# A second product in two nested levels of seven-for-eight block products, its weight operands streamed from DRAM

## Chip, cores, metric

One core of a Trainium2 chip runs the whole kernel. The metric is device time in microseconds (us). "Before" is the kernel before the change, "after" the changed kernel.

## The reference

```python
batch, m, k, h, n = 16, 512, 768, 3072, 768          # 8192 rows of x
y = np.matmul(x, w1) + b1
y = 0.5 * y * (1.0 + erf(y / np.sqrt(2.0)))          # GELU
return np.matmul(y, w2).astype(np.float32)
```

Two dense products with a GELU between them. Operands are float16 on the chip, sums float32.

## The kernel before

The rows are worked on in eight blocks of 1024. In each block the first product gives G = gelu(x w1 + b1), and the second gives G w2. Each product is cut into 2 x 2 quarters and made with seven quarter products instead of eight (the scheme of Strassen and Winograd). VectorE makes the sums and differences of operands that the seven products need, and VectorE and ScalarE combine the seven results as they leave PSUM. A "unit" is one set of seven products that share the PSUM banks bX, bY, bZ and bW.

The first product has 12 units a block, each of 7 x 3 matmuls of 512 columns. The second has 4 units, each of 7 x 12 matmuls of 384 columns:

```python
class Unit2:                                # second product, 128 + 128 rows a unit
    F = N2                                  # 384 columns
    C = NH                                  # 12 chunks of the contraction
    def mm(self, p, dst, first, c0, c1):
        ...
        for c in range(c0, c1):
            a = {1: G1[:, c, 0, r], 2: G2[:, c, 0, r], 4: G2[:, c, 1, r],
                 3: GS[3][:, c, :], 5: GS[0][:, c, :], 6: GS[1][:, c, :],
                 7: GS[2][:, c, :]}[p]
            nc.tensor.matmul(out=dst[:, 0:N2], lhsT=a, rhs=w2o[:, slot, c, :], ...)
```

All of w2 and its sums (`w2o`) stays in SBUF. The pieces of w1 are loaded again in every block with a cast on the way, by DMAs that POOL issues, and their sums are made again by VectorE. x is loaded by POOL and turned by DMA transposes that SP issues. These run during the second product of the block before:

```python
# in the second product, unit k, between products ("slots")
if k == 0 and slot == 4:  # load x tiles 0-3 of the next block
if k == 1 and slot == 1:  # DMA-transpose them
if k == 1 and slot == 4:  # load tiles 4-7, and four pieces of w1 (POOL)
if k == 2 and slot == 1:  # transpose tiles 4-7
```

Of the kernel before, what the change touches and what calls it, by code (L numbers as in the profile page):

```python
# [14 lines left out]
PSUM = bass.MemoryType.PSUM  # L15

# [14 lines left out]
def kernel(  # L31
# [25 lines left out]

    wp = ctx.enter_context(tc.tile_pool(name="wp", bufs=1))
    wtp = ctx.enter_context(tc.tile_pool(name="wtp", bufs=4))
    xhp = ctx.enter_context(tc.tile_pool(name="xhp", bufs=4))  # L60
    pwp = ctx.enter_context(tc.tile_pool(name="pwp", bufs=2))
    tmpp = ctx.enter_context(tc.tile_pool(name="tmpp", bufs=2))
    outp = ctx.enter_context(tc.tile_pool(name="outp", bufs=2))
    pp = ctx.enter_context(tc.tile_pool(name="pp", bufs=1, space=PSUM))

    w2o = wp.tile([P, 7, NH, N2], F16, name="w2o")
    G1 = wp.tile([P, NH, 2, RH], F16, name="G1")
    G2 = wp.tile([P, NH, 2, RH], F16, name="G2")
    GS = [wp.tile([P, NH, P], F16, name=f"GS{k}") for k in range(4)]
    XT = wp.tile([P, 2, 2 * KQ, RH], F16, name="XT")  # L70
    XS = [wp.tile([P, KQ, RH], F16, name=f"XS{k}") for k in range(4)]
# [9 lines left out]
    with tc.manual_schedule():  # L81

        soon, queue, late = [], [], []
# [20 lines left out]

        def load_wt(n):
            hi = n % NH
            wt = wtp.tile([P, 7, KQ, P], F16, name="wt")
            wts[n] = wt
            for half in range(2):
                c0 = (half * NH + hi) * P  # L110
                nc.gpsimd.dma_start(  # L111
                    out=wt[:, 2 * half:2 * half + 2, :, :].rearrange("p a k c -> p (a k) c"),
                    in_=w1r[:, :, c0:c0 + P])
# [7 lines left out]

        def prep_wt(n):
            wt = wts[n]
            t_ops(lambda s: wt[:, s, :, :], KQ * P, soon)

        W2C = 3

        def load_w2(q, c):
            slot, r0, n0 = ((B11, 0, 0), (B21, NH, 0), (T1, 0, N2), (B22, NH, N2))[q]
            nc.gpsimd.dma_start(out=w2o[:, slot, c:c + W2C, :],  # L130
                                in_=w2r[:, r0 + c:r0 + c + W2C, n0:n0 + N2])

        def prep_w2(c):
            t_ops(lambda s: w2o[:, s, c:c + W2C, :], W2C * N2, queue, late)
# [3 lines left out]
        def load_x(sb, t):  # L138
            xh = xhp.tile([P, K], F16, name="xh")
            nc.gpsimd.dma_start(out=xh[:], in_=xr[:, sb * 8 + t, :])  # L140
            xhs[t] = xh
# [4 lines left out]
        def transpose_dma(t):  # L146
            nc.sync.dma_start_transpose(out=xT_of(t), in_=xhs[t][:])
# [15 lines left out]
        def x_sums():  # L163
            n = KQ * RH
            later(n, lambda: tt(XS[0][:], A21, A22, ADD))
            later(n, lambda: tt(XS[1][:], XS[0][:], A11, SUB))
            later(n, lambda: tt(XS[2][:], A11, A21, SUB))
            later(n, lambda: tt(XS[3][:], A12, XS[1][:], SUB))

        def g_sum(k, u, c0=0, c1=NH):  # L170
# [5 lines left out]
            later((c1 - c0) * P, lambda: tt(s[k], a, b, op))  # L176


        class Unit1:
# [4 lines left out]
            def __init__(self, g, sb, hi):  # L184
                self.g, self.sb, self.hi = g, sb, hi
                self.wt = wts[sb * NH + hi]
# [9 lines left out]
            def alloc(self):  # L196
                self.tmp = tmpp.tile([P, 2, RH], FP32, name="tmp")
# [7 lines left out]
            def right_done(self):  # L205
                hi = self.hi
                nc.scalar.activation(out=G2[:, hi, :, :], in_=self.tmp[:], func=GELU,  # L207
                                     bias=b1t[:, NH + hi:NH + hi + 1])
# [6 lines left out]
        class Unit2:  # L215
# [7 lines left out]
            def mm(self, p, dst, first, c0, c1):  # L223
                r = slice(self.u * P, (self.u + 1) * P)
                slot = {1: B11, 2: B21, 3: B22, 4: T4, 5: T1, 6: T2, 7: T3}[p]
                for c in range(c0, c1):
# [3 lines left out]
                    nc.tensor.matmul(out=dst[:, 0:N2], lhsT=a, rhs=w2o[:, slot, c, :],  # L230
# [3 lines left out]
            def alloc(self):  # L234
                self.o = outp.tile([P, 2, N], FP32, name="osb")
# [15 lines left out]

        def p1(u, c0, c1):
            u.mm(1, bX[u.g % 2], True, c0, c1)
# [3 lines left out]

        def p7(u):
            u.mm(7, bY[u.g % 2], False, 0, u.C)

        def add_c22(u):
            nc.vector.tensor_tensor(out=u.c22(), in0=bY[u.g % 2][:, 0:u.F],  # L262
                                    in1=u.pw[:, 0:u.F], op=ADD)
# [3 lines left out]

        def copy_w(u):
            u.pw = pwp.tile([P, 512], FP32, name="pw")
            nc.scalar.copy(out=u.pw[:, 0:u.F], in_=bW[:, 0:u.F])  # L270
# [3 lines left out]

        def add_c12(u):
            nc.vector.tensor_tensor(out=u.c12(), in0=bZ[:, 0:u.F], in1=u.pw[:, 0:u.F], op=ADD)  # L276
            u.right_done()
# [7 lines left out]

        def copy_yz(u):
            nc.vector.tensor_copy(out=bZ[:, 0:u.F], in_=bY[u.g % 2][:, 0:u.F])  # L287
# [6 lines left out]
        def period(i, j, fill):  # L294

            turn = isinstance(i, Unit2) and isinstance(j, Unit1)
            if turn:
                p7(j)
                add_c22(j)
                p1(i, 0, 5)  # L300
                p3(j)
                add_c12(j)
# [4 lines left out]
            else:  # L307
# [3 lines left out]
                if j:  # L311
                    p7(j)
                    add_c22(j)
            fill(1)
            if i:
                p5(i)
                copy_w(i)
            fill(2)
            if j and not turn:
                p3(j)  # L320
                add_c12(j)
            fill(3)
            if i:
                p6(i)
                copy_yz(i)
# [32 lines left out]
        x_sums()  # L358
# [4 lines left out]

        units = []
        for sb in range(nsb):
            units += [(1, sb, hi) for hi in range(NH)] + [(2, sb, u) for u in range(NU)]
        w2_loads = [(q, c) for c in range(0, NH, W2C) for q in range(4)]
        prev = None
        for g, (kind, sb, k) in enumerate(units):
            last_sb = sb + 1 == nsb  # L370

            def fill(slot, kind=kind, sb=sb, k=k, last_sb=last_sb):
                if kind == 1:
                    n = sb * NH + k
                    if slot == 1:
                        if k in (5, 9):
                            for s in range(4):
                                g_sum(s, 0, k - 5, k - 1)
                        if k == NH - 1:
                            for s in range(4):  # L380
                                g_sum(s, 0, 8, 10)
                        if k + 1 < NH:
                            prep_wt(n + 1)
                        if sb == 0 and k >= 3 and k % 2 == 1 and (k - 3) // 2 * W2C < NH:
                            prep_w2((k - 3) // 2 * W2C)
                        sums(900)
                    if slot == 4:
                        sums(1500)
                    if slot == 5 and k >= 1 and k + 3 < NH:
                        load_wt(n + 3)  # L390
                    if slot == 5 and sb == 0:
                        for q, c in w2_loads[:2]:
                            load_w2(q, c)
                        del w2_loads[:2]
                    if slot == 6:
                        flush(soon)
                        if k == NH - 1:
                            flush(queue)
                else:
                    if slot == 1:  # L400
                        if k == 0:
                            for s in range(4):
                                g_sum(s, 0, 10, NH)
                        else:
                            g_sum(2, k)
                        flush(queue)
                    if slot == 2 and k + 1 < NU:
                        queue.extend(late)
                        late.clear()
                        g_sum(0, k + 1)  # L410
                    if slot == 3 and k > 0:
                        g_sum(3, k)
                    if slot == 4 and k + 1 < NU:
                        g_sum(1, k + 1)
                    if slot > 1:
                        sums(1200)
                    if not last_sb:
                        if k == 0 and slot == 4:
                            for t in range(4):
                                load_x(sb + 1, t)  # L420
                        if k == 1 and slot == 1:
                            for t in range(4):
                                transpose_dma(t)
                        if k == 1 and slot == 4:
                            for t in range(4, 8):
                                load_x(sb + 1, t)
                            for n in range(4):
                                load_wt((sb + 1) * NH + n)
                        if k == 2 and slot == 1:
                            for t in range(4, 8):  # L430
                                transpose_dma(t)
                        if k == 3 and slot == 2:
                            prep_wt((sb + 1) * NH)
                            x_sums()
                    if slot == 6 and k == NU - 1:
                        flush(queue)
                        flush(soon)

# [34 lines left out]
```

## Time and profile before

| | before |
|---|---|
| median of 3 runs | 905.48 us (905.38 to 906.16) |
| TensorE matmul (PE) busy | 98% of a span of 904.5 us |
| VectorE (DVE), ScalarE (ACT) busy | 58%, 43% |
| mean granted TensorE clock | 0.992 |

Two stretches of the trace, one first product and one second product in the middle of the run. Columns: the stretch, then busy time of each engine with its number of instructions, the granted clock as a share of full speed, the mean busy share of the 16 DMA engines, and GB/s. The DMA share adds up the packets' times, which can overlap, so it can pass 1.

```profile
core 0: us, PE busy (x) PEld busy (x) DVE busy (x) ACT busy (x) POOL busy (x), PEclk, DMA share, GB/s
245.00:299.00 54.00, 54.00 (x255) 24.79 (x254) 39.45 (x89) 37.58 (x57) 15.29 (x20) 1.00 0.75 88
299.00:354.00 55.00, 55.00 (x336) 32.68 (x334) 24.83 (x41) 10.12 (x20) 8.71 (x12) 1.00 0.72 115
```

PE is busy all the time in both. In the second product VectorE is idle for more than half of it, and the DMA engines for about a quarter.

The timeline of PE at the end of the last block shows how far apart the matmuls start: 12 of 384 columns start every 1.95 us.

```profile
888.41 2.11 PE L230 MATMUL bY_93<-w2o,GS_80 128*128 128x384 f16 x12
890.36 2.11 PE L230 MATMUL bY_92<-w2o,G_78 128*128 128x384 f16 x12
```

From such starts, 162.5 ns for 384 columns and 215.9 ns for 512, I take 2.5 ns + 0.417 ns a column. For each pair of neighbouring matmuls, the distance of their starts less this figure is "excess". For the kernel before, the figures add up to 877.9 us and the excess to 21.0 us, 20.5 of it in the start-up and the first block. From the second block on almost nothing is lost: TensorE alone sets the time.

### The profile page before, as it was taken

How to read it: one execution, taken by the hardware profiler on the slowest of the kernel's cores; microseconds unless marked ns; L12 is line 12 of the kernel's file. 1: busy time of each engine (PE TensorE's matmuls, PEld its weight loads, DVE VectorE, ACT ScalarE, POOL GpSimd, SP SyncE). 2: the span in 40 equal slices, each digit the busy share in tenths (PEclk: the TensorE clock that was granted, in tenths of full speed). 3: DMA queues.
4: the chain of work that ended last, by engine and by line, in shares of the span. 5: the costliest groups of instructions: out<-in, count | busy, mean ns of one | idle time of the engine just before them, and what ended most of it. 6: DMA issues, size and time to landing. Idle time of an engine off the chain costs nothing.

```text
span 904.5 us, 12591 instructions
## 1 busy us (share of the span) xinstructions
PE 886.6 (98%) x4764; PEld 465.6 (51%) x4764; DVE 529.0 (58%) x1045; ACT 386.2 (43%) x614; POOL 204.9 (23%) x278
## 2 busy tenths in 40 slices
PE   5999999999999999999999999999999999999998
PEld 2444654456544565445654466544654456544564
DVE  3788446854578436774267734676346764468532
ACT  2665116741177312772137721476115751167411
POOL 5561202321033300333003230132302412022000
PEclk7999999999999999999999999999999999999999
DMA  9997916969179881979439692497915979168011
GB/s 156 119 194 118 160 59 88 98 105 164 56 86 105 102 143 71 88 88 145 100 86 89 89 169 76 79 92 99 169 71 78 87 107 166 54 90 85 1 70 70
DMA packets 223308, 92.06 MB, mean 102 GB/s; under 512 B 200720, under 2 KB 215056, under 8 KB 223248
## 3 DMA queue, kind: packets, MB, share of 16 engines
q0 software_dynamic: 166144, 55.07, 56.1%
q1 hardware_dynamic: 57104, 36.20, 14.9%
q8 instruction: 37, 0.61, 0.3%
q14 instruction: 23, 0.19, 0.1%
HBM read 110.11 MB, written 25.17 MB: 150 GB/s over the span
## 4 chain that ended last, share of the span: by engine, by line
PE 92%; DMA 5%; DVE 1%; POOL 1%; issue 1%; ACT 0%; DVEq 0%; POOLq 0%
PE bY_93 L230 10%; PE bY_92 L230 10%; PE bY_93 L192 9%; PE bY_92 L192 9%; PE bX_90 L230 7%; PE bZ L230 7%; PE bX_91 L230 7%; PE bW L230 7%; PE bW L192 6%; PE bZ L192 6%; PE bX_91 L192 6%; PE bX_90 L192 6%; DMA wt<-in_w_dram 3%; DMA xh<-in_x_dram 1%; DVE wt L86 1%
## 5 line engine op out<-in xcount | busy, mean ns | idle before, releaser
L192 PEld LDWEIGHTS <-wt 128*128 128x128 f16 x2016 | 197.6, 98 | 245.2 <-issue 11.2
L111 POOL DMA_DIRECT2D wt<-in_w_dram x192 | 158.0, 837 | 489.3 <-PE bY_92 L192 344.4
L207 ACT ACTIVATE G_78<-tmp,b1t 128x1024 f16<-128x1024 f32 x96 | 110.2, 1148 | 123.8 <-DVE tmp L276 123.8
L86 DVE TENSOR_TENSOR wt<-wt 128x384 f16<-128x384 f16 x384 | 135.6, 353 | 10.2 <-DMA wt<-in_w_dram 3.3
L270 ACT COPY pw<-bW 128x512 f32<-128x512 f32 (+1 forms) x128 | 71.8, 561 | 112.2 <-PE bW L230 88.4
L230 PEld LDWEIGHTS <-G_78 128*128 128x128 f16 x768 | 75.2, 98 | 50.4
L192 PE MATMUL bW<-XS_84,wt 128*128 128x512 f16 x288 | 78.5, 382 | 4.0 <-DVE wt L86 4.0
L192 PE MATMUL bX_90<-XT,wt 128*128 128x512 f16 x288 | 78.9, 383 | 0.0
L192 PE MATMUL bX_91<-XT,wt 128*128 128x512 f16 x288 | 77.8, 379 | 0.0
L192 PE MATMUL bZ<-XS_87,wt 128*128 128x512 f16 x288 | 77.8, 379 | 0.0
L276 DVE TENSOR_TENSOR tmp<-bZ,pw 128x512 f32<-128x512 f32 x96 | 65.7, 684 | 5.6 <-PE bZ L192 5.6
L262 DVE TENSOR_TENSOR tmp<-bY_92,pw 128x512 f32<-128x512 f32 x48 | 33.2, 691 | 59.4 <-PE bY_92 L192 38.7
L230 PE MATMUL bW<-w2o,GS_79 128*128 128x384 f16 x384 | 67.6, 326 | 0.0
L230 PE MATMUL bZ<-w2o,GS_82 128*128 128x384 f16 x384 | 67.6, 326 | 0.0
L140 POOL DMA_DIRECT2D xh<-in_x_dram x64 | 34.6, 551 | 136.8 <-DMA XT<-xh 116.4
L262 DVE TENSOR_TENSOR osb<-bY_92,pw 128x384 f32<-128x384 f32 x16 | 8.9, 558 | 85.9 <-issue 82.8
L287 DVE COPY bZ<-bY_92 128x512 f32<-128x512 f32 (+1 forms) x64 | 42.6, 666 | 17.3 <-PE bY_92 L230 11.2
L230 PEld LDWEIGHTS <-G_77 128*128 128x128 f16 x384 | 37.6, 98 | 27.4
L262 DVE TENSOR_TENSOR tmp<-bY_93,pw 128x512 f32<-128x512 f32 x48 | 33.0, 688 | 31.4 <-PE bY_93 L192 23.5
L230 PEld LDWEIGHTS <-GS_81 128*128 128x128 f16 x384 | 37.6, 98 | 25.6
L230 PEld LDWEIGHTS <-GS_82 128*128 128x128 f16 x384 | 37.6, 98 | 25.6
L230 PEld LDWEIGHTS <-GS_80 128*128 128x128 f16 x384 | 37.6, 98 | 24.8
(58 smaller groups left out, 1128.5 us busy)
## 6 DMA issues: line engine op xcount, KB each, us to landing
wt<-in_w_dram POOLq DMA_DIRECT2D x192, 192.0 KB, 4.6
out_dram<-osb SPq DMA_DIRECT2D x64, 384.0 KB, 2.3
xh<-in_x_dram POOLq DMA_DIRECT2D x64, 192.0 KB, 5.4
w2o<-in_w_dram POOLq DMA_DIRECT2D x16, 288.0 KB, 8.7
XT<-xh SPq DMA_TRANSPOSE x56, 3.8
b1t<-in_b_dram SPq DMA_DIRECT2D x1, 12.0 KB, 5.3
```

The costliest lines, as they stand in the source:

```text
L86: nc.vector.tensor_tensor(out=o, in0=a, in1=b, op=op)
L111: nc.gpsimd.dma_start(out=wt[:, 2 * half:2 * half + 2, :, :].rearrange("p a k c -> p (a k) c"), in_=w1r[:, :, c0:c0 + P])
L140: nc.gpsimd.dma_start(out=xh[:], in_=xr[:, sb * 8 + t, :])
L192: nc.tensor.matmul(out=dst[:, 0:RH], lhsT=self.wt[:, slot, c, :], rhs=a[:, c, :], start=first and c == 0, stop=c == self.C - 1, skip_group ...
L207: nc.scalar.activation(out=G2[:, hi, :, :], in_=self.tmp[:], func=GELU, bias=b1t[:, NH + hi:NH + hi + 1])
L230: nc.tensor.matmul(out=dst[:, 0:N2], lhsT=a, rhs=w2o[:, slot, c, :], start=first and c == 0, stop=c == self.C - 1, skip_group_check=True)
L262: nc.vector.tensor_tensor(out=u.c22(), in0=bY[u.g % 2][:, 0:u.F], in1=u.pw[:, 0:u.F], op=ADD)
L270: nc.scalar.copy(out=u.pw[:, 0:u.F], in_=bW[:, 0:u.F])
L276: nc.vector.tensor_tensor(out=u.c12(), in0=bZ[:, 0:u.F], in1=u.pw[:, 0:u.F], op=ADD)
L287: nc.vector.tensor_copy(out=bZ[:, 0:u.F], in_=bY[u.g % 2][:, 0:u.F])
```

## The change

The intent is to save matmul time in the second product. From block 3 on, each of its seven quarter products is again cut in four and made with seven products: 49 products of 12 matmuls of 192 columns, 588 x 192 columns where there were 336 x 384. Blocks 1 and 2 keep the old form. During them the 49 operands of w2 are stored in DRAM: VectorE makes 28 of them, and 21 are pieces of operands that were there already. From block 3 on they are streamed through a ring of 15 buffers, 15 loaded during the first product and 34 while the second runs. The pieces of w1 with their sums are kept in DRAM too, and loaded ready-made by SP. To make room, most SBUF buffers are now laid over each other in one `arena`.

The core of the diff (cuts marked):

```diff
+    w1s = [dp.tile([P, 7, KQ, P], F16, name=f"w1s{n}") for n in range(NH)]        # DRAM
+    w2s = {(p, q): dp.tile([P, NQ, N4], F16, name=f"w2s{p}{q}") ...}              # DRAM, 49
+    RING = 15
...
+            if hi in kept:                                   # load_wt, from block 3 on
+                nc.sync.dma_start(out=wt[:], in_=w1s[hi][:])
+                return
...
+        def load_ring(sb, n):
+            if n < 49 and sb < nsb:
+                nc.sync.dma_start(out=ring_of(sb, n), in_=w2s[w2_order[n]][:])
...
+        class Unit3:                                         # 7 of these a block
+            def mm(self, q, dst, first, c0, c1):
+                for c in range(NQ):
+                    for t in range(2):
+                        nc.tensor.matmul(out=dst[:, t * N4:(t + 1) * N4], lhsT=a,
+                                         rhs=w[:, c, :], ...)  # 192 columns
+                load_ring(self.sb, n + RING)
...
+                if self.p == 5:                              # fourth unit
+                    for r in range(2):
+                        tt(par[1][:, r], par[1][:, r], self.dst[:, r], ADD)
+                    for r in range(2):
+                        nc.gpsimd.tensor_tensor(out=self.dst[:, r], in0=par[2][:, r],
+                                                in1=self.dst[:, r], op=ADD)
+                        self.store(r)
...
+            if sb + 1 < nsb:                                 # second product, unit k
+                if k == 0 and slot == 1: load_next_x(sb + 1, range(3))
+                if k == 1 and slot == 4: # DMA-transpose tiles 0-2, load 3-5
+                if k == 3 and slot == 1: # DMA-transpose tiles 3-5, load 6-7
+                if k in (4, 5, 6) and slot == 6:
+                    load_wt((sb + 1) * NH + k - 4)           # first weights of the next block
+                if k == 4 and slot == 4: # DMA-transpose tiles 6-7
```

## The prediction

> **What bounds the kernel now.** TensorE. The page shows PE busy 98% of 904.5 us and granted clock 0.992; the chain that ended last is 92% PE. The timeline of PE shows matmuls packed without gaps: 12 of 384 columns start every 1.95 us (162.5 ns each), 3 of 512 columns every 0.648 us (215.9 ns each). That fits 2.5 ns + 0.417 ns a column. A 1024-row block is 252 matmuls of 512 columns (54.4 us) and 336 of 384 (54.6 us), 109.0 us together, which is also the distance from block to block in the timeline. VectorE 58%, ScalarE 43%, DMA are hidden.
>
> **What the change does.** In blocks 3 to 8 (six of eight) the second product takes 49 products of 12 matmuls of 192 columns: 588 per block instead of 336. My estimate from the fit is 82.5 ns each, 48.5 us a block, so 6.1 us saved per block and 36.5 us in all. This needs each weight load to hide behind only 82.5 ns of streaming. The trace's warm transposes (128 columns, one load each) start about 55 ns apart, but only six in a row. The Trainium skill, "TensorE: Matmul & The Clock Gate", section "Back-to-back issue gap", gives about 81 ns sustained for load and matmul pairs at 128 columns; no run here shows that yet. If true it is just not binding at 192.
>
> **Added costs.**
> - VectorE. The 48 weight sums a block (0.353 us) vanish from block 3 on, and the old activation sums (about 16 us). New, at 0.95 us per 1536 elements: 28 level sums (27 us), half sums and S4 (about 14 us), and five of seven units with six 384-wide evictions of 0.56 us (about 19 us with the rest). About 50 us of that must run inside the 48.5 us second product, about 84 us a block. So VectorE becomes nearly as full as TensorE there; I expect 0 to 3 us of stalls a block, chiefly where the second product begins and ends.
> - DMA. A ring load is 128 x 2304 B. Stores of 3072 B packets took 125 ns (packet times in the trace), so about 95 ns by proportion, 0.76 us per load on 16 engines, against 0.99 us per product. With x loads, transposes and first weights the second product asks for slightly more than the engines' whole time (share about 1.1), but 15 products of prefetch are made in the first product, which absorb a backlog of some 8. First-product weights become large plain loads instead of casting ones (837 ns of POOL each now); that relieves the DMA.
> - Blocks 1 and 2: 28 more splits of about 0.75 us and 49 stores fit VectorE's idle half. The first block's first product already has DMA share 1.18 and loses 2.7 us (stretch view); narrower w2 pieces add about 2 us. Earlier x loads give back about 1 us.
>
> **Sum.** 905.5 - 36.5 + about 6 (VectorE, turns) + about 2 (blocks 1 and 2) = 877 us, 80% between 867 and 891. Faster by over 2% (below 887.4): 0.78; within 2%: 0.18; slower: 0.04.
>
> **What would show it.** 192-column matmuls start 82 to 84 ns apart in the PE timeline; block distance 103 to 105 us from block 3 on; VectorE over 85% busy in those second products, PE waits there naming VectorE lines, few naming the ring's DMA; POOL busy falls by over half.
>
> **What would make it wrong.** Pair pitch above 90 ns (weight load or issue bound): 588 x 7.5 ns x 6 = 26 us lost, gain gone. Ring loads late because stores or transposes sit in front of them in SP's in-order queue (a transpose holds SP about 1.3 us). VectorE's order delaying evictions that free PSUM banks, in every period rather than at the turns.

## The result

The changed kernel takes 932.19 us (median of 4 runs, 928.63 to 933.76) against 905.50: ratio 1.0288, 95% interval 1.0257 to 1.0318. A ratio here is the mean time of one kernel's fast runs over that of the other's of the same rounds, so it is not quite the ratio of the medians. The prediction was 877 us with 867 to 891: wrong, and in the wrong direction.

| | before | after |
|---|---|---|
| span of the profiled run | 904.5 us | 929.7 us |
| sum of matmul figures (2.5 ns + 0.417 ns a column) | 877.9 us | 841.3 us |
| excess | 21.0 us | 82.7 us |
| mean granted clock | 0.992 | 0.977 |

The saving of 36.6 us is there, exactly as estimated. It is overrun by 61.7 us of excess: blocks 4 to 8 begin 111 to 114 us after the block before, where 103 to 105 were predicted. The PE timeline of block 3 shows both (start, us, engine, line, operation, tiles, shapes, count, and in brackets the idle time before it and what ended it):

```profile
350.57 1.15 PE L422 MATMUL bY_144<-arena,G_134 128*128 128x192 f16 x12
351.56 1.15 PE L422 MATMUL bX_143<-arena,G_134 128*128 128x192 f16 x12
352.55 1.15 PE L422 MATMUL bX_142<-arena 128*128 128x192 f16 x12
355.04 1.15 PE L422 MATMUL bY_145<-arena 128*128 128x192 f16 x12 [1.33 <-DVE bZ L515]
...
366.40 1.46 PE L333 MATMUL bX_143<-XT,wt 128*128 128x512 f16 x3 [5.27 <-DMA wt<-w1s_72]
367.66 2.13 PE L422 MATMUL bY_144<-arena 128*128 128x192 f16 x12
369.58 1.49 PE L333 MATMUL bW<-XS_136,wt 128*128 128x512 f16 x3
```

Twelve matmuls start in 0.99 us, 82.5 ns each, with a weight load for every one. Then there is a gap in which PE waits for VectorE's sum into bank bZ, and at the turn into block 4 one of over 5 us in which it waits for the first weights of that block. After it the same twelve matmuls take 1.92 us between starts: TensorE runs at half clock.

PE's waits, longest sums first (us in total, times, longest):

```profile
PE bX_143 L333 <- DMA wt<-w1s_72: 12.9, 3, 5.3
PE bX_142 L333 <- DMA wt<-w1s_72: 8.8, 2, 5.9
PE bY_145 L422 <- DVE bZ L515: 5.4, 6, 1.3
PE bY_144 L422 <- DVE bZ L515: 5.4, 6, 1.3
PE bY_144 L371 <- ACT bY_144 L475: 5.1, 1, 5.1
```

From the starts of the matmuls the 61.7 us of added excess come to:

| where | added us | how counted |
|---|---|---|
| gaps at the turns into blocks 4 to 8 | 22.6 | 5.43 + 3.07 + 5.16 + 6.10 + 2.79 |
| half clock right behind those gaps | 9.4 | 2.40 + 1.30 + 1.46 + 2.71 + 1.56 |
| waits for VectorE in the second and sixth unit, six blocks | 12.8 | 6 x 0.63 and 6 x 1.5 |
| blocks 1 and 2, gaps and half clock | 13.3 | block 3 begins at 252.6 us against 239.3; 5.3 of it one gap in block 2's second product |
| rest of blocks 3 to 8 | 3.6 | remainder |

(The expectations below call the unit of the second wait the fifth. Counted from one, as the second unit is, it is the sixth.)

Why are the weights late? SP's timeline of the later part of block 3's second product (start, us for the issue, what):

```profile
335.20 7.53 SPq L255 DMA_TRANSPOSE XT<-xh  x3
...
350.23 3.33 SPq L255 DMA_TRANSPOSE XT<-xh  x2
353.65 0.55 SPq L239 DMA_DIRECT2D arena<-w2s_99  x1
354.29 1.41 SPq L446 DMA_DIRECT2D out_dram<-arena  x2
355.80 0.49 SPq L239 DMA_DIRECT2D arena<-w2s_104  x1
356.34 0.47 SPq L157 DMA_DIRECT2D wt<-w1s_72  x1
```

In the program the request for the first weights stands right behind the fifth unit's last product, and TensorE was through with that at 345.6 us. SP comes to it 10.7 us later: five transposes held it for 7.53 and 3.33 us, and between them it waited 1.8 us for an x tile. The chain that ended last then has this load as one link of ten microseconds (start, us, link):

```profile
356.34 10.02 DMA wt<-w1s_72
```

Two things are wrong at once. The load is issued only at 356.3 us, when PE needs it at about 361. And it takes 10 us instead of the 4 us that such loads take in the middle of the first product. The stretches of the same block, cut as for the kernel before, show the reason for the latter:

```profile
260.00:311.00 51.00, 51.00 (x239) 23.20 (x238) 31.90 (x54) 38.71 (x61) 0.00 (x0) 1.00 0.60 207
311.00:360.00 49.00, 47.07 (x551) 45.41 (x550) 46.57 (x80) 12.94 (x25) 9.09 (x10) 1.00 0.99 257
...
365.00:371.00 6.00, 4.60 (x19) 2.84 (x20) 0.56 (x1) 0.57 (x1) 0.00 (x0) 0.50 1.04 399
```

In the second product VectorE went from 24.8 us busy to 46.6 of 49, and the DMA engines from a share of 0.72 to 0.99. In slices of 6 us the share is 0.38 at first, and 1.03 to 1.17 from 323 us on. In the first product it is 0.60.

The last line, six microseconds right behind the gap, shows the granted clock at 0.50. The Trainium skill, "TensorE: Matmul & The Clock Gate", section "What's actually happening", says that the clock falls to half after an idle window of about 3.4 us. The traces here agree on the 3.4 us, but show that less idle time is enough. In all sixteen traces the stretches of half clock that do not run into the end of the kernel last 3.41 us or a whole multiple of it (6.83, 13.65), and those at the five turns of this kernel begin 112.64 us apart (364.53, 477.17 and so on), which is 33 slots of 3.413 us. With all traces cut into such slots, and the first 25 us left out, full clock was lost after each of the 44 slots in which PE was idle for 1.98 us or more, and after none of the 4026 with 1.97 us or less (idle by the modelled ends of matmuls). So what a gap costs depends on where it falls: one that left PE idle for 2.04 us in e14_pet_late was followed by half clock, one of 3.5 us in e13_notr_late, cut in two by the edge of a slot, was not.

### The profile page after: what moved, and what is told of

It is laid out like the page before. It is cut to its first block, busy times and chain, and to the rows that moved or that the text cites. A ratio compares the mean times of both kernels' runs of the same rounds, so it can differ in the third digit from the quotient of the medians.

```text
span 929.7 us, 16276 instructions
## 1 busy us (share of the span) xinstructions
PE 869.7 (94%) x6276; PEld 565.6 (61%) x6276; DVE 665.6 (72%) x1151; ACT 417.1 (45%) x680; POOL 116.4 (13%) x146
## 4 chain that ended last, share of the span: by engine, by line
PE 66%; DMA 15%; DVE 12%; ACT 2%; issue 2%; POOL 1%; SPq 1%; DVEq 0%; ACTq 0%; POOLq 0%
PE bY_144 L333 9%; PE bY_145 L333 8%; PE bX_143 L333 6%; DVE arena L127 6%; PE bW L333 5%; PE bX_142 L333 5%; PE bZ L333 5%; DMA wt<-in_w_dram 4%; DMA wt<-w1s_72 4%; PE bY_145 L422 4%; PE bY_144 L422 4%; PE bW L422 3%; PE bZ L422 3%; PE bX_142 L422 2%; PE bX_143 L422 2%
## 5 line engine op out<-in xcount | busy, mean ns | idle before, releaser
L422 PEld LDWEIGHTS <-arena 128*128 128x128 f16 x2664 | 226.0, 99 | 21.1 <-issue 16.6
L348 ACT ACTIVATE G_134<-arena,b1t 128x1024 f16<-128x1024 f32 x96 | 110.3, 1149 | 63.8 <-DVE arena L505 63.8
L127 DVE TENSOR_TENSOR arena<-arena 128x1536 f16<-128x1536 f16 (+5 forms) x176 | 127.7, 746 | 0.9
L482 DVE TENSOR_TENSOR arena<-bY_145,pw 128x512 f32<-128x512 f32 (+1 forms) x52 | 35.4, 681 | 94.9 <-PE bY_145 L333 69.0
L333 PE MATMUL bX_143<-XT,wt 128*128 128x512 f16 x288 | 80.1, 388 | 13.1 <-DMA wt<-w1s_72 12.9
L333 PE MATMUL bX_142<-XT,wt 128*128 128x512 f16 x288 | 80.5, 389 | 8.8 <-DMA wt<-w1s_72 8.8
L505 DVE TENSOR_TENSOR arena<-bZ,pw 128x512 f32<-128x512 f32 (+1 forms) x104 | 70.5, 678 | 19.6 <-PE bZ L333 13.8
L333 PE MATMUL bY_144<-XT,wt 128*128 128x512 f16 x288 | 78.0, 379 | 3.5 <-DVE bZ L520 3.4
L482 DVE TENSOR_TENSOR arena<-bY_144,pw 128x512 f32<-128x512 f32 (+1 forms) x52 | 35.4, 681 | 63.1 <-PE bY_144 L333 35.8
L333 PE MATMUL bY_145<-XT,wt 128*128 128x512 f16 x288 | 77.8, 379 | 2.1 <-DVE bZ L520 1.2
L475 ACT COPY bY_145<-bX_143 128x512 f32<-128x512 f32 (+1 forms) x73 | 39.9, 547 | 83.3 <-DVE arena L454 39.5
L475 ACT COPY bY_144<-bX_142 128x512 f32<-128x512 f32 (+1 forms) x73 | 40.4, 554 | 69.8 <-DVE arena L454 39.6
L422 PE MATMUL bY_144<-arena 128*128 128x192 f16 x612 | 61.7, 253 | 5.4 <-DVE bZ L515 5.4
L422 PE MATMUL bY_145<-arena 128*128 128x192 f16 x612 | 60.5, 250 | 5.4 <-DVE bZ L515 5.4
L371 PEld LDWEIGHTS <-arena 128*128 128x128 f16 x384 | 38.0, 99 | 32.3 <-issue 7.0
L127 DVE TENSOR_TENSOR arena<-arena,G_133 128x1024 f16<-128x1024 f16 (+4 forms) x86 | 48.5, 564 | 1.8
L161 POOL DMA_DIRECT2D wt<-in_w_dram x48 | 39.5, 831 | 79.8 <-DVE wt L127 35.3
```

The lines of the kernel that those rows point to most:

```text
L127: nc.vector.tensor_tensor(out=o, in0=a, in1=b, op=op)
L161: nc.gpsimd.dma_start(out=wt[:, 2 * half:2 * half + 2, :, :].rearrange("p a k c -> p (a k) c"), in_=w1r[:, :, c0:c0 + P])
L333: nc.tensor.matmul(out=dst[:, 0:RH], lhsT=self.wt[:, slot, c, :], rhs=a[:, c, :], start=first and c == 0, stop=c == self.C - 1, skip_group ...
L348: nc.scalar.activation(out=G2[:, hi, :, :], in_=self.tmp, func=GELU, bias=b1t[:, NH + hi:NH + hi + 1])
L422: nc.tensor.matmul(out=dst[:, t * N4:(t + 1) * N4], lhsT=a, rhs=w[:, c, :], start=first and c == 0 and t == 0, stop=c == NQ - 1, skip_grou ...
L475: nc.scalar.copy(out=bY[u.g % 2][:, 0:u.F], in_=bX[u.g % 2][:, 0:u.F])
```

## The experiments

The theories. BANDWIDTH: the DMA engines have too little time in the second product, and whatever is moved, something waits. ORDER: the first weights are late because they stand last in SP's queue. VECTORE FULL: VectorE is the limit there. PORT: POOL's additions slow VectorE.

| run | edit | result | us | ratio to before | 95% |
|---|---|---|---|---|---|
| e1_early | first weights early | correct | 916.5 | 1.0121 | 1.0096 to 1.0147 |
| e2_act | first weights by ScalarE's queue | correct | 964.6 | 1.0638 | 1.062 to 1.0656 |
| e3_noadd | no additions on POOL | wrong | 928.5 | 1.0245 | 1.0222 to 1.0268 |
| e4_actstore | stores of blocks 1, 2 by ScalarE's queue | correct | 933.1 | 1.0312 | 1.0264 to 1.0359 |
| e6_halfring | e1, half of each streamed operand | wrong | 897.4 | 0.9893 | 0.9871 to 0.9915 |
| e7_notr | e1, no DMA transposes | wrong | 897.5 | 0.9896 | 0.9879 to 0.9914 |
| e5_pet | e1, transposes on TensorE | correct | 902.0 | 0.9946 | 0.9928 to 0.9964 |
| e8_dve | e1, VectorE work moved | correct | 916.3 | 1.0105 | 1.0086 to 1.0124 |
| e13_notr_late | no DMA transposes, weights late | wrong | 923.7 | 1.018 | 1.0154 to 1.0206 |
| e10_mix | e1, 5 of 8 transposes on TensorE, block 2 relieved | correct | 926.4 | 1.0205 | 1.0168 to 1.0242 |
| e11_mix_dve | e10 and e8 | correct | 923.5 | 1.0177 | 1.015 to 1.0205 |
| e12_petblock2 | e5, block 2 relieved | correct | 898.5 | 0.9901 | 0.9881 to 0.9922 |
| e14_pet_late | transposes on TensorE, weights late | correct | 910.7 | 1.004 | 1.0022 to 1.0057 |
| e15_pb2_dve | e12 and e8 | correct | 902.5 | 0.9951 | 0.9934 to 0.9967 |

The record counts ratios within 2% of 1 as the same. Where a smaller difference is called faster below, it is because its interval leaves out 1.

### e1_early: the first weights at the start of the second product

```diff
-                if k in (4, 5, 6) and slot == 6:
-                    load_wt((sb + 1) * NH + k - 4)
+                if k == 0 and slot in (2, 4, 6):
+                    load_wt((sb + 1) * NH + slot // 2 - 1)
```

> The first three weight loads of the next block are issued at the start of the second product (its first period) instead of behind its last ring loads, transposes and stores. Nothing else changes; the bytes are the same. Theory ORDER (the loads are late because they stand last in SP's queue, while the DMA engines have free time in the first 12 us of the second product, shares 0.38 and 0.83): the five gaps of 2.8 to 6.1 us at the start of the first product, 22.6 us together, and about 9 us of half clock behind them go; no wait for ring loads appears; about 900 us. Theory BANDWIDTH (the engines lack time in the second product as a whole, share 1.0 to 1.2): PE then waits for ring loads or later weight loads instead, and the time stays above 920 us.

Measured 916.5 us, between the two ranges and nearer the second. All waits for first weights are gone. In their place PE waits for ring loads, which it does not do in the kernel after. PE's waits in this run:

```profile
PE bX L422 <- DMA arena<-w2s: 10.0, 9, 2.0
PE bY L422 <- DVE bZ L515: 7.7, 10, 1.5
PE bY L422 <- DMA arena<-w2s: 5.5, 8, 1.2
```

So of the 32 us at the turns (22.6 of gaps, 9.4 of half clock) about half, 15.7 us, went with the order alone: the bytes are the same. The other half came back as waits for other loads, which is what BANDWIDTH expects. These waits are short, at most 2 us, and no half clock follows any of them.

### e2_act: the same loads through another engine's queue

```diff
-                    load_wt((sb + 1) * NH + k - 4)
+                    load_wt((sb + 1) * NH + k - 4, nc.scalar)
```

> The same three weight loads at their old place in the program, but issued by ScalarE's queue. ORDER in the sense of SP's in-order queue alone: they leave 2 to 5 us earlier and do not stand behind SP's transposes and stores, the gap at the turn falls to under 1 us, about 905 us. BANDWIDTH: they still take about 10 us to land because the DMA engines are full, the gap falls by 1 to 3 us a turn only, 915 to 927 us.

Measured 964.6 us; neither theory expected it to be slower. Its profiled run is slow (978.9 us), its three timed runs are 963 to 965. In that profile PE now waits up to 15.8 us for a ring load at the turn, and 10.6 us for ScalarE's copies into bank bY (L475), which cost nothing at this place in the kernel after:

```profile
PE bX L422 <- DMA arena<-w2s: 51.0, 5, 15.8
PE bY L422 <- ACT bY L475: 10.6, 5, 3.2
```

The chain at 343 to 351 us shows how: such a copy stands behind a weight-load instruction in ScalarE's stream, and that instruction is held until 350.0 us. Around the long wait the DMA engines are busy and move little:

```profile
354.00:360.00 6.00, 6.00 (x75) 5.99 (x73) 3.49 (x7) 0.94 (x2) 0.00 (x0) 1.00 0.88 81
366.00:372.00 6.00, 0.00 (x0) 0.00 (x0) 0.60 (x1) 0.00 (x0) 0.72 (x2) 0.50 1.03 170
```

In the packet records of 345 to 380 us, transpose packets took up to 2.7 us (median 18 ns) and weight packets of the second queue up to 4.4 us (median 206 ns), while transposes and these loads ran side by side. That the two streams hold each other up is what I read from it; no run took them apart, so the cause of the long waits for ring loads stays open. The Trainium skill, "DMA: Bandwidth & Descriptors", section "Issuing engines are not separate DMA queues", says that DMAs of all issuing engines run on the same 16 DMA engines, so that a second issuer gains only issue time. This run agrees that it gained nothing in transfer time, and shows a loss that the section does not mention.

### e3_noadd: without POOL's additions (wrong result)

```diff
-                        nc.gpsimd.tensor_tensor(out=self.dst[:, r], in0=par[2][:, r],
-                                                in1=self.dst[:, r], op=ADD)
```

> Wrong result on purpose: POOL's two additions of 768 elements in the fourth unit of each second product are left out, their stores remain. Theory PORT (POOL's additions slow VectorE's neighbours from 0.95 us to 1.6 and 2.1 us, and that makes the gap of 1.5 us in the fifth unit): that gap falls below 0.3 us in all six blocks, about 8 us less with the turns unchanged, 922 to 925 us. Theory VECTORE FULL (the queue of VectorE work is too long there with or without POOL): the gap stays above 1 us.

In the kernel after, VectorE's timeline in block 3 shows the operations beside POOL's two additions (347.5 to 352.4 us), and the one just behind them:

```profile
349.05 1.64 DVE L127 TENSOR_TENSOR arena<-arena 128x1536 f16<-128x1536 f16 x1
...
351.08 2.10 DVE L127 TENSOR_TENSOR arena<-arena 128x1536 f16<-128x1536 f16 x1
...
353.56 0.94 DVE L127 TENSOR_TENSOR arena<-arena 128x1536 f16<-128x1536 f16 x1
```

In e3_noadd the operation that took 2.10 us:

```profile
348.25 0.95 DVE L127 TENSOR_TENSOR arena<-arena 128x1536 f16<-128x1536 f16 x1
```

Without the additions these operations take 0.95 us, and the gap of 1.5 us in the sixth unit falls below 0.7 us in all blocks; what is left there waits for ring loads. PORT is right about the gap (the Trainium skill, "GPSIMD Engine Reference", section "Specifications", says that POOL shares its SBUF interfaces with VectorE and contends with instructions that have two SBUF inputs; the trace agrees, with 0.95 us against 1.64 and 2.10). But the time fell by only 3.7 us and not by the 8 expected, and the intervals of the two kernels overlap: the gaps at the turns stay (22.4 us in sum), and ring loads now come late by 0.4 to 1.5 us. What VectorE gave back was mostly hidden behind the other limit.

### e4_actstore: the stores of blocks 1 and 2 through ScalarE's queue

```diff
-                nc.sync.dma_start(out=orr[:, self.sb * 8 + self.u, :], in_=self.o[:, 0, :])
+                nc.scalar.dma_start(out=orr[:, self.sb * 8 + self.u, :], in_=self.o[:, 0, :])
...  # the second store likewise
```

> The output stores of blocks 1 and 2 are issued by ScalarE's queue instead of SP's, where in block 2 one stood behind transposes, four weight loads of 672 KB and the stores of the split weights and took 12.3 us, holding the one output buffer. ORDER: the gap of 5.3 us in block 2's second product goes, with 1.4 us of half clock, 924 to 927 us. BANDWIDTH: the store still takes over 10 us and the gap stays.

Measured 933.1 us, no change within the noise. The gap of 5.3 us in block 2's second product is gone, and a new one of 5.7 us stands at the turn into block 3, where the chain leads over the last x loads and DMA transposes (6.28 us to landing). In block 2 too, letting one transfer pass moved the wait to the next.

### e6_halfring and e7_notr: less DMA work (both give a wrong result)

```diff
# e6_halfring, on top of e1_early
-                nc.sync.dma_start(out=ring_of(sb, n), in_=w2s[w2_order[n]][:])
+                nc.sync.dma_start(out=ring_of(sb, n)[:, 0:NQ // 2, :],
+                                  in_=w2s[w2_order[n]][:, 0:NQ // 2, :])
# e7_notr, on top of e1_early, in the second products from block 3 on
-                        transpose_dma(t)
+                        pass
```

> Wrong result on purpose: on top of e1_early, every streamed weight operand is loaded only by half (3 of its 6 chunks), so the ring's DMA time in a second product falls by about 13 us; the instructions of all engines stay. BANDWIDTH (the DMA engines lack time in the second product as a whole): all DMA waits of blocks 3 to 8 go, the VectorE gaps of 0.6 and 1.5 us and 0.3 at the turn stay, 895 to 902 us. ORDER (the waits left in e1_early come from what stands in front in SP's queue: transposes and stores): most of them stay, above 908 us.

> Wrong result on purpose: on top of e1_early, the eight DMA transposes of each second product from block 3 on are left out. They fill the engines with 256-byte packets for about 12 us a block (share 0.74 to 0.9 in the slices where they run) and hold SP for 18 us. BANDWIDTH and ORDER both expect the DMA waits of blocks 4 to 8 to go, 895 to 902 us; if the ring's bytes alone were the matter the time would stay above 908 us.

Measured 897.4 and 897.5 us. Two quite different cuts of about the same engine time (my estimate from the packet times: 11.8 and 10.6 us of each second product) give the same result, and leave nearly the same list of waits. This is e6_halfring's; no line of it names a ring load or a first weight:

```profile
PE bY L422 <- DVE bZ L515: 10.8, 12, 1.3
PE bY L371 <- ACT bY L475: 5.0, 1, 5.0
PE bT L259 <- DMA G<-in_x_dram: 4.9, 6, 2.6
PE bY L333 <- DVE bZ L520: 4.2, 8, 0.9
```

BANDWIDTH holds for what e1_early had left. It is e6_halfring that decides this, because it leaves SP's instructions as they were; leaving the transposes out frees SP's queue too (14.5 us in block 3 of the kernel after, not the 18 of the expectation), so e7_notr and e5_pet alone could not tell the two theories apart. Leaving the transposes out has a side effect: POOL's x loads no longer wait for transposes to free their buffers, so they all run ahead to the turn. In e7_notr that did no harm, in e13_notr_late below it did.

### e5_pet: the transposes on TensorE

```diff
+                t = {(1, 4): 0, (1, 5): 1, (1, 6): 2, (3, 1): 3, (3, 2): 4, (3, 3): 5,
+                     (4, 4): 6, (4, 5): 7}.get((k, slot))
+                if t is not None:
+                    transpose_pe(t, True)      # 6 matmuls of 128 columns, ScalarE evicts
-                # the three groups of DMA transposes; x loads follow their tiles
```

> On top of e1_early, the transposes of the second product from block 3 on are made by TensorE (48 of 128 columns a block, about 56 ns each by the start-up's trace, 2.7 us a block) and evicted by ScalarE, instead of the DMA engines. If the transposes' DMA time is what pushes the second product over the engines' limit, the DMA waits of e1_early go (about 18 us) and 5 x 2.7 us of TensorE come back: 908 to 913 us, with gaps of VectorE alone. If it is not, 925 us or more.

Measured 902.0 us, better than expected, with the right result: this is faster than the kernel before by 0.5% (interval 0.4 to 0.7). The timeline of PE shows the price, 0.33 us for the six matmuls of a tile, 2.65 us a block:

```profile
319.49 0.50 PE L259 MATMUL bT<-ident,xh 128*128 128x128 f16 x6
319.82 1.15 PE L422 MATMUL bY<-arena,G 128*128 128x192 f16 x12
```

No wait for ring loads or first weights is left, and in blocks 3 to 7 the VectorE gaps shrink to one of 0.83 us. That VectorE's work now has 2.65 us more time a block is the likely reason; no run shows it by itself. The DMA engines are relieved where it matters: from 341 us on their share is 0.82 where e1_early has 1.12 (e5_pet first, then e1_early):

```profile
341.00:365.00 24.00, 23.34 (x270) 21.89 (x268) 22.06 (x33) 5.59 (x10) 6.46 (x5) 1.00 0.82 250
```

```profile
341.00:365.00 24.00, 18.76 (x218) 17.71 (x216) 20.78 (x29) 2.93 (x6) 7.04 (x7) 1.00 1.12 296
```

### e8_dve: VectorE's work moved into the first product

```diff
-                    half_sums(slice(m, m + NQ + 1, NQ), (0, 1, 2) if m < 4 else (0, 1))
-                    if k == 9:
-                        lev_sums(1, 0, 3); lev_sums(2, 0, 3)
+                    half_sums(slice(m, m + NQ + 1, NQ))
+                    if k == 11:
+                        lev_sums(1, 3, 5); lev_sums(2, 3, 5)
+                elif k == 8:
+                    lev_sums(1, 0, 3); lev_sums(2, 0, 3)
...  # and taken out of the second product's first unit
```

> On top of e1_early, 3.4 us of VectorE's level sums a block move from the start of the second product into the last units of the first product. Theory VECTORE FULL: the gaps of 0.63 and 1.5 us in the second and fifth unit fall below 0.5 us together, but as long as the DMA engines are the limit the blocks get shorter by less than 1.5 us each: 908 to 916 us. If VectorE alone set the remaining time, 903 us or less.

Measured 916.3 us against e1_early's 916.5: nothing, at the upper end of what BANDWIDTH expects. The gap of 0.63 us in the second unit turned into one of 0.72 us at the turn into the second product.

### e13_notr_late: does order matter by itself? (wrong result)

```diff
# the kernel after, weights late as there
-                        transpose_dma(t)
+                        pass
```

> Wrong result on purpose: the changed kernel as it was handed over (first weights still last in SP's queue), only without the eight DMA transposes of each second product from block 3 on. BANDWIDTH alone: with 12 us of engine time a block given back the late loads land in time, the gaps of 2.8 to 6.1 us at the turns into blocks 5 to 8 fall below 0.5 us each, about 900 us. ORDER also needed: gaps of 2 to 4 us stay at the turns, with half clock behind them, 908 to 918 us.

(The turns meant are those into blocks 4 to 8.) Measured 923.7 us, with gaps of up to 4 us at four of the five turns. But the run does not prove what it was made for. POOL's x loads run ahead, all eight of them to the turn (the first four of them):

```profile
349.00 4.88 POOL L467 TENSOR_TENSOR arena<-arena 128x768 f32<-128x768 f32 x2 [94.11 <-DVE arena L127]
353.83 1.63 POOL L248 DMA_DIRECT2D xh<-in_x_dram  x3
359.51 0.53 POOL L248 DMA_DIRECT2D xh<-in_x_dram  x1 [4.05 <-DMA xh<-in_x_dram]
```

The late weights met the x loads there, so order and crowding are mixed. e14_pet_late repeats the test without that.

### e14_pet_late: the fourth corner

```diff
# e5_pet's transposes on TensorE, on the kernel after (weights late as there)
```

> The changed kernel as handed over (first weights last in SP's queue), with the transposes of the second product from block 3 on made by TensorE as in e5_pet. The fourth corner of the square of (transposes on DMA or TensorE) x (weights late or early): 932, 916, 902 and this. If engine time is the whole cause and order only decides who waits: the gaps at the turns fall below 0.5 us and it is 901 to 905 us. If order matters by itself: gaps of 2 us and more stay at the five turns with half clock behind them, 910 to 920 us.

Measured 910.7 us, just inside the second range. But the gaps are not the ones expected: only the turn into block 4 has one above 2 us with half clock behind it, three others have 0.5 to 0.9 us, and the last has none. The square of medians:

| | weights late | weights early |
|---|---|---|
| DMA transposes | 932.2 (after) | 916.5 (e1_early) |
| TensorE transposes | 910.7 (e14_pet_late) | 902.0 (e5_pet) |

Both causes are real and partly overlap: early weights are worth 15.7 us with DMA transposes and 8.7 us without them, and taking the transposes off the DMA engines is worth 21.5 or 14.5 us, although it puts 13 us of work on TensorE (5 x 2.65). The corners come from different rounds, in which the kernel before took 905.5 to 907.8 us; from the ratios the four worths are 1.7, 0.9, 2.5 and 1.8% of its time. Of the 8.7 us that early weights are worth without DMA transposes, the two profiled runs put about 6.5 at the turns and 2.4 in blocks 1 and 2, where the kernels are alike. SP's timeline before the turn into block 4, and the link of the chain of waits:

```profile
350.95 2.88 SPq L446 DMA_DIRECT2D out_dram<-arena  x2
353.92 1.36 SPq L239 DMA_DIRECT2D arena<-w2s  x1
355.33 0.45 SPq L157 DMA_DIRECT2D wt<-w1s  x1
```

```profile
355.33 8.85 DMA wt<-w1s
```

The DMA share of this run falls to 0.66 in 345 to 350 us and 0.36 in 350 to 355. The engines had time; SP had not yet reached the load, which stands behind stores that wait for POOL's two additions (348.53 to 353.41 us). Once issued, it met full engines again (share 1.06 and 1.03 in 355 to 365) and took 8.85 us. So order is at work here without the transposes, though not without bandwidth.

### e10_mix, e11_mix_dve, e12_petblock2, e15_pb2_dve: towards a version that beats both

e12_petblock2 is e5_pet, with block 2 relieved in the same way: eight transposes on TensorE and four early weight loads in its second product. e10_mix is the same with only five of eight tiles on TensorE from block 3 on, the first three by DMA. e11 and e15 add e8's move of VectorE work to e10 and e12.

```diff
+            if sb == 1:                                       # block 2
+                t = {(1, 2): 0, (1, 3): 1, (1, 4): 2, (2, 2): 3, (2, 3): 4, (2, 4): 5,
+                     (3, 1): 6, (3, 2): 7}.get((k, slot))
+                if t is not None:
+                    transpose_pe(t, True)
...  # x loads follow
+                if (k, slot) in ((0, 2), (0, 4), (0, 6), (1, 1)):
+                    load_wt(2 * NH + (slot // 2 - 1 if k == 0 else 3))
```

> A version meant to beat both: early weight loads; from block 3 on the first three of the eight transposes stay with the DMA engines and five go to TensorE (about 1.7 us a block instead of 2.7); in block 2 all eight go to TensorE and the next block's four weight loads are issued at the start of its second product. Expected against e5_pet: 5 us less TensorE time, block 2's gap of 5 us and its half clock gone, 2.7 us of TensorE more there: 892 to 898 us, correct result. If three DMA transposes already overfill the engines, DMA waits come back and it is 900 us or more.

> e10_mix with e8_dve's shift of 3.4 us of VectorE work a block into the first product. With the DMA waits gone VectorE's gaps (0.6 and 0.8 to 1.5 us a block) count now: 3 to 8 us less than e10_mix if VECTORE FULL is what is left; the same within 2 us if the shift only moves the gap to the turn.

> e5_pet (all eight transposes on TensorE from block 3 on) with the same relief of block 2: 5 us gap and about 1.9 us of half clock go, 2.7 us of TensorE come: about 897 to 899 us, correct result. Against e10_mix it tells whether three DMA transposes a block are free (e10_mix 4 to 5 us faster) or cost DMA waits (e10_mix not faster).

> e12_petblock2 with e8_dve's shift of 3.4 us of VectorE work a block into the first product. VECTORE FULL with the DMA waits gone: the gaps left in e12_petblock2 from block 3 on (0.83 us in the fifth unit, 0.6 and 1.5 us in the last block) fall by half or more, 2 to 5 us less: 893 to 897 us. If the shift only moves the wait to the turn, 898 to 900 us.

e10_mix was a miss: 926.4 us. The ring does not run dry; TensorE itself waits for an x tile that it is to transpose. The x loads of tiles 3 to 5 wait for the three DMA transposes (6.7 us under load), and land after PE has come to their transposes, in the middle of its in-order stream:

```profile
437.52 1.15 PE L422 MATMUL bY<-arena 128*128 128x192 f16 x12
443.03 0.51 PE L259 MATMUL bT<-ident,xh 128*128 128x128 f16 x6 [4.36 <-DMA xh<-in_x_dram]
```

So it tells nothing about whether three DMA transposes are free; it shows that my placing of the others was too early for the buffers there are. e11_mix_dve, 923.5 us, has the same fault.

e12_petblock2 is the best version: 898.5 us, as expected, with the right result, 1.0% under the kernel before (interval 0.8 to 1.2) and 3.6% under the kernel after (898.5 over 932.2). The gap in block 2 is gone and no wait of over 1 us is left in the second products of blocks 3 to 7. e15_pb2_dve, 902.5 us, lies outside both of its ranges: it keeps the gap of about 0.8 us a block and adds one of 0.7 in the second product's first units. The move of VectorE work made a wait and took none away.

## Why the prediction was wrong

- The saving. Predicted 36.5 us from 82.5 ns a matmul; measured 36.6 us, and 82.5 ns to the digit. This step was right. The worry of weight loads or issue being the bound was unfounded: twelve loads hide behind twelve matmuls of 192 columns.
- VectorE. Predicted "nearly as full as TensorE" and "0 to 3 us of stalls a block"; measured 46.6 us of 49 busy and 2.1 us of gaps a block (12.8 us in all). Right in kind and size, though the sum took only "about 6" for it and the turns together. The run without POOL's additions shows that at least 0.8 us of the 2.1 comes from POOL slowing VectorE, which I had not counted.
- DMA. The prediction had the right load: 0.76 us a ring load from 95 ns a packet (measured median 93 ns), "share about 1.1" (measured 1.03 to 1.17 from 12 us into the second product on). The step that failed is its conclusion, "15 products of prefetch are made in the first product, which absorb a backlog of some 8". The ring did absorb it: PE never waited for a ring load in the kernel after. But the engines' backlog does not belong to the ring. It falls on whatever is asked for last and has no prefetch, and that was the first weights of the next block, issued by SP behind the ring, the transposes and the stores. 22.6 us of gaps and 9.4 us of half clock stand where the sum had about 6 for the turns and VectorE together. e1_early, e6_halfring, e7_notr, e5_pet and e14_pet_late show both halves: too much DMA work in the second product, and the wrong order of it.
- Half clock. Not in the prediction at all. 9.4 us at the turns, set off by gaps that left PE idle for 2.6 to 5.9 us: waits cut into pieces of at most 2 us, as in blocks 3 to 8 of e1_early, cost none of it.
- Blocks 1 and 2. Predicted "about 2" us; measured 13.3. Half of it has the same reason as at the turns: the added stores of operands, the weight loads and the transposes delay an output store (12.3 us to landing), and there is one output buffer. That gap and its half clock are about 7 us, and are gone in e12_petblock2; the rest is spread over short waits and was not taken apart.
- "What would make it wrong" did name "ring loads late because stores or transposes sit in front of them in SP's in-order queue". The right queue and the wrong victim.

What stays open: why PE waits so long for ring loads when ScalarE's queue issues the first weights, and whether some of the eight transposes can stay with the DMA engines at no cost.

## What to carry to other kernels

When a change turns resident operands into streamed ones, add up the DMA engines' time for the stage, not for the run, and then ask who stands last in the queue: a prefetch ring protects only its own stream, and the backlog goes to the one without prefetch. An early request for the next stage's first operands, made while the engines were still free, was worth 8.7 to 15.7 us here. And where TensorE has just been given back time, some of it may buy more than it costs: 13 us of transposes on TensorE took 14.5 to 21.5 us off the kernel.

## What the Trainium skill lacked or had wrong

- "TensorE: Matmul & The Clock Gate", section "Back-to-back issue gap", gives about 131 ns sustained for load and matmul pairs at 512 columns and 81 ns at 128. Here pairs of 512 columns start 215.9 ns apart, of 384 162.5, of 192 82.5, and of 128 (the transposes) 55 ns in groups of six; each follows 2.5 ns + 0.417 ns a column to within 1 ns, with nothing added for the weight load. That is the figure which the same section gives for an isolated matmul only.
- The same page, section "What's actually happening", asks for an idle window of about 3.4 us before the clock falls. In the runs here 1.98 us of idle time within one slot of 3.413 us were enough, and 1.97 were not.
- "DMA: Bandwidth & Descriptors", section "Latency and other measured facts", gives 261 GB/s for DMA transposes, measured on one kernel. Here a tile of 128 x 768 float16 (196,608 bytes) took 1.19 us of all 16 engines before (66.7 us for 56 tiles in the packet records), about 165 GB/s, and 1.41 us after, about 139 GB/s. Other transfers ran beside them, so this is what the transposes got here and not what they could reach. SP was held about 1.3 us a tile before, and 2.5 us on average for three in a row (7.53 us) after.
- The same page, section "Issuing engines are not separate DMA queues", does not say that moving loads to a second issuer can cost time. Here it did, 965 us against 932: ScalarE's copies waited behind the load instructions (10.6 us), and single packets of that queue took up to 4.4 us against a median of 206 ns (slow profiled run, cause open).
- No page read here gives a figure for what the backlog of full DMA engines does to a kernel whose streams are issued in program order by one engine. Here it was 10 us for a load of 672 KB at a DMA share above 1, 4 us for the same load where the share was 0.6.
